# Seven of 22 up-projection pairs as seven products, low parts of weights partly by DMA, and the down projection's weight sums made earlier

## The chip, the cores and the metric

The kernel runs on one core of a Trainium2 chip. The metric is device time in microseconds (us) of one execution. A core has five engines that run their own instruction streams side by side: TensorE (PE, matrix products), VectorE (DVE), ScalarE (ACT), GpSimd (POOL) and SyncE (SP, here only the issuer of loads). They wait for one another by semaphores. Data moves between memory (DRAM) and the on-chip buffers by 16 DMA engines; SP, ACT and POOL issue such transfers, each on its own queue. A PE product lands in one of eight banks of the accumulation memory.

## The reference

One layer of an encoder: x is 512 tokens of 1024 numbers in float32, with 256 memory tokens. Cut to its steps:

```python
h = rmsnorm(x, pre_mix_g)
aq, ak, av, hq, hf_fwd, hf_bwd, hi, hg = split_columns(h @ w_in, IN_SPLITS)
att = axial_gqa_attention(apply_rope(rmsnorm(aq, q_norm_g)), apply_rope(rmsnorm(ak, k_norm_g)), av)
rec = hgrn2_group(hq, hf_fwd, hf_bwd, hi, hg, lb, hg_out_norm_g)   # a scan over the tokens, both directions
x = x + rmsnorm(concatenate([att, rec]) @ w_out, post_mix_g)
h, m = rmsnorm(x, pre_x_g), rmsnorm(mem, mem_norm_g)
x = x + rmsnorm(memory_cross_attention(h, m, w_xq, w_xkv, w_xo), post_x_g)
u = rmsnorm(x, pre_ffn_g) @ w_up                                   # 1024 -> 2 * 2816
gate, val = split(conv_b + sum(pad(u)[j:j + 512] * conv_w[j] for j in range(3)))
x = x + rmsnorm((silu(gate) * val) @ w_down, post_ffn_g)           # 2816 -> 1024
```

## The kernel before

**Products in three.** Every float32 product is made of three matmuls in the format float32r. An operand is split into a high part (a cast) and a low part (the rest); `mm3` (L242 to L245) multiplies high by high, high by low and low by high into one bank. `split` (L117 to L119) makes the two parts: an ACT cast (L118) and a DVE subtraction (L119).

**Weights come in units.** A unit is a block of 128x1024 numbers (512 KB); there are 162, numbered in the order in which PE uses them. Units 0 to 65 belong to the token mixing and the cross attention, 66 to 119 to the up projection, 120 to 161 to the down projection. `load_w` issues a unit's load on SP. `issue` makes the unit's high part `wh` and low part `wl`, up to three units ahead of use (AHEAD); each has four buffers, so a unit's parts can be made only when the unit four places earlier has been used. Most low parts are DVE subtractions. For units 7 to 30 (NEG_SCALAR) ACT writes the negated high part into `wl` (L214), and POOL issues a DMA that adds the weight to it from memory (L217). For units 31 to 41 (NEG_POOL) POOL does the negation (L216).

**Attention.** The token mixing runs a scan over chunks of tokens on DVE (L633, L639), ACT (L604) and PE (L607, bank c), and between its steps the planner puts products of the attention. `turn_k` (L711 to L716) transposes the keys of one block of 128 tokens on PE into a bank with the tag b and has ACT cast the result out (L716). The attention projection's products use bank b too. A tag stands for two banks that take turns.

**Residual and norm.** `between` (L309 to L325) adds a sub-layer's normed output to x, norms the sum and hands back a call of `turn_in` (L278 to L289), which transposes the result on PE and splits it for the next projection. Before the up projection it also keeps an unsplit copy of each transposed block in `fulls` (ACT, L289).

**Up projection.** The 22 pairs of a gate block and a value block run in a loop over i. A plain pair is two units, each 24 matmuls of 128x512. A pair named in UP_S uses a scheme of seven half-size products in place of eight (Strassen's): 84 matmuls of 128x256. It takes four units: `diag` and `side` are loaded, `sums` and `last` are sums of blocks of these made by `add_blocks` on DVE, where `both` holds the double sum. The left operands are sums of the halves of h, made by `sum_of_h` from `fulls` during pairs 2 and 3.

**Down projection.** It uses seven products p = 0 to 6 as well, with six units each. Four of the seven weights are sums of blocks of w_down (t1 to t4). `new_sums` (L988 to L999) makes them in DRAM, at every third pair of the up projection: a copy of the first block (on ACT's queue L997 or POOL's L994) and an adding DMA of the second (L998, POOL). The loads for the down projection wait for them. The left operands are the products of gate and value, in three groups g of eight pairs or six; `left_side` (L1010 to L1027) splits the operand of product p for group g, either on ACT and DVE, or, for the (p, g) in NEG_GROUP, by an ACT cast (L1022), a POOL negation (L1023) and an adding DMA between on-chip buffers (L1024). For p = 3 a DVE subtraction (L1014) first overwrites what the earlier operand was split from. `order` runs through p and, within it, g; LAY_AHEAD = 3 of them are laid ahead.

A tile framework places the buffers and semaphores: an instruction waits until its inputs are written and until the earlier users of its output's buffer are done.

Of the kernel before, what the change touches and what calls it, by code (L numbers as in the profile page):

```python
# [9 lines left out]
F32 = mybir.dt.float32  # L10
# [8 lines left out]
P = 128  # L19
# [9 lines left out]
UP_S = (5, 8, 11, 14, 17)  # L29
# [6 lines left out]
SUMS = (("t1", "w11", "w12"), ("t3", "w22", "w12"), ("t2", "t1", "w22"), ("t4", "t2", "w21"))  # L36
BLOCKS = ("w11", "w12", "w21", "w22")
UP_PRODUCTS = ("w11", "w22", "t2", "w21", "t1", "t3", "t4")
LAY_AHEAD, LOAD_AHEAD = 3, 5
SIDES_AT = (18, 19)  # L40
NEG_GROUP = frozenset((p, 1) for p in (1, 2, 5, 6))
# [3 lines left out]
NEG_SCALAR = frozenset(range(7, 31))  # L45
# [41 lines left out]
def layer(tc, io, out):  # L87
# [42 lines left out]
    issued, loaded, taken, last_load, rooms = [0], [0], [0], [None], [0]  # L130
# [12 lines left out]
    whole = N_MIX  # L143
    for i in range(NF):
        if i in UP_S:
            plan += [(kind, UP_S.index(i)) for kind in ("diag", "side", "sums", "last")]
        else:
            plan += [("w", whole), ("w", whole + 1)]
            whole += 2
# [16 lines left out]

    def load_w():
        i = loaded[0]
        loaded[0] += 1
        if i >= N_DOWN:  # L170
            p, u = divmod(i - N_DOWN, 6)
            cols = width(u)
            raw = raw_room(i)[:, :cols.stop - cols.start]
            src = weight_block(PRODUCTS[p][0], cols)
        else:
            kind, n = plan[i]
            if kind in ("sums", "last"):
                return None
            raw = raw_room(i)
            src = io["w"][n] if kind == "w" else io["wu"][n, ("diag", "side").index(kind)]  # L180
        last_load[0] = nc.sync.dma_start(raw, src).ins
        return raw

    def add_blocks(kind, raw, ahead):
        if kind == "diag":
            both = vp.tile([P, 1024], F32, name="both", tag="vv")
            mid = ahead[:, :512]
            nc.vector.tensor_tensor(out=both.rearrange("p (a n) -> p a n", a=2), in0=raw.rearrange("p (a n) -> p a n", a=2),
                                    in1=mid[:, None, :].to_broadcast([P, 2, 512]), op=ALU.add)
# [8 lines left out]
    def issue():  # L198
# [12 lines left out]
        if i in NEG_SCALAR or i in NEG_POOL:  # L211
            nc.scalar.copy(wh, raw)  # L212
            if i in NEG_SCALAR:
                nc.scalar.mul(wl, wh.bitcast(F32), -1.0)  # L214
            else:
                nc.gpsimd.tensor_scalar(wl, wh.bitcast(F32), -1.0, 0.0, op0=ALU.mult, op1=ALU.add)  # L216
            nc.gpsimd.dma_start(wl, io["w"][i], accum_op=ALU.add)  # L217
        else:
            split(wh, wl, raw)
            add_blocks(kind, raw, raws[0] if raws else None)  # L220
        pending.append((wh, wl))

    hold = [N_UNITS]

    def issue_ahead():
        while issued[0] < min(hold[0], taken[0] + AHEAD):
            issue()
        while N_MIX + 4 <= taken[0] and loaded[0] < min(N_UNITS, taken[0] + LOAD_AHEAD):
            raws.append(load_w())
# [48 lines left out]
    def turn_in(h, act, b, tags, keep=None):  # L278
        for c in range(2):
# [8 lines left out]
            if keep:  # L288
                nc.scalar.copy(keep[c][:, :, blk(b)], o)  # L289
# [19 lines left out]
    def between(x, g_post, g_pre, act, keep=None):  # L309
# [4 lines left out]
        def second(b, got, y):  # L314
# [9 lines left out]
            return lambda: turn_in(h, act, b, y_tags[0][b] + y_tags[1][b], keep)  # L324
# [83 lines left out]
    nhalf = const.tile([P, 16], F32, name="nhalf")  # L408
    warm = tmp2()
# [301 lines left out]
    def turn_k(b):  # L711
        o = bank("b").rearrange("p (k n) -> p k n", k=4)
# [270 lines left out]
    fulls = [big([P, 4, T]) for _ in range(2)]  # L983
    turns = res_second(ox, range(4), kv["x0"], between(x, g_post, g_pre, hT, fulls))
# [78 lines left out]
    for part in range(2):  # L1063
        cols = slice(part * 256, part * 256 + 256)
        for n in range(4):
# [10 lines left out]
    of_h = [(s1, a21, a22), (s2, a11, s1), (s3, a21, a11), (s4, a12, s2)]  # L1076

# [47 lines left out]
    for i in range(2, NF):  # L1125
        if i in UP_S:
            strassen_pair(i)
        else:
            for c in range(2):
# [183 lines left out]
```

## Time and profile before

| | us |
|---|---|
| median of 3 runs | 825.16 |
| the three runs | 825.16, 825.99, 824.77 |
| profiled execution | 825.72 |
| its span, first to last instruction | 823.8 |

The granted PE clock was 0.999 of full speed. The time of a run is about 1.9 us longer than the span that the trace covers; positions below are us from the span's start. In rows of the trace the columns are: start, duration, engine, line of the kernel, operation, output<-input, shape, and in brackets the idle time of the engine before it with what ended that. A row of the list of waits has the waiting engine, its output and line, what it waited for, and total us, number and longest. A row of busy time by stage has, for a stretch of the span, the busy us of PE, PE's weight loads, DVE, ACT and POOL (with the number of instructions), the granted PE clock, the busy share of the DMA engines and GB/s. In a row of the costliest groups the number behind an x counts the instructions, and then come their busy us and the mean ns of one. The up projection runs from about 484 to 709 us, the down projection from 709 to 816.

### The profile page before, as it was taken

How to read it: one execution, taken by the hardware profiler on the slowest of the kernel's cores; microseconds unless marked ns; L12 is line 12 of the kernel's file. 1: busy time of each engine (PE TensorE's matmuls, PEld its weight loads, DVE VectorE, ACT ScalarE, POOL GpSimd, SP SyncE). 2: the span in 40 equal slices, each digit the busy share in tenths (PEclk: the TensorE clock that was granted, in tenths of full speed). 3: DMA queues.
4: the chain of work that ended last, by engine and by line, in shares of the span. 5: the costliest groups of instructions: out<-in, count | busy, mean ns of one | idle time of the engine just before them, and what ended most of it. 6: DMA issues, size and time to landing. Idle time of an engine off the chain costs nothing.

```text
span 823.8 us, 11495 instructions
## 1 busy us (share of the span) xinstructions
PE 808.1 (98%) x4354; PEld 690.6 (84%) x4354; DVE 568.5 (69%) x849; ACT 473.0 (57%) x785; POOL 132.3 (16%) x194
## 2 busy tenths in 40 slices
PE   9999999999999999999999999999999999999996
PEld 7878888889898887888888898889889888878884
DVE  5347486569886875855453769787687796868865
ACT  6666756369788874645543665444344453556651
POOL 0110211044233101300001300111110102100302
PEclk9999999999999999999999999999999999999999
DMA  9696753657668533252212145787898885368842
GB/s 316 186 283 134 173 112 95 129 140 162 160 155 191 116 136 120 77 179 78 88 43 101 37 163 153 205 232 202 224 279 217 232 250 146 103 200 295 249 124 102
DMA packets 39671, 135.66 MB, mean 165 GB/s; under 512 B 5120, under 2 KB 6656, under 8 KB 39424
## 3 DMA queue, kind: packets, MB, share of 16 engines
q1 hardware_dynamic: 25632, 86.03, 30.0%
q0 software_dynamic: 10960, 40.38, 25.5%
q10 hardware_dynamic: 3024, 8.53, 2.9%
q8 instruction: 34, 0.56, 0.3%
q14 instruction: 21, 0.17, 0.1%
HBM read 130.72 MB, written 25.17 MB: 189 GB/s over the span
## 4 chain that ended last, share of the span: by engine, by line
PE 84%; DMA 4%; DVE 4%; issue 3%; ACT 2%; POOL 2%; SPq 0%; POOLq 0%; DVEq 0%; ACTq 0%
PE ps_b L243 9%; PE ps_b L244 9%; PE ps_b L245 9%; PE ps_s L244 6%; PE ps_s L245 6%; PE ps_s L243 6%; PE ps_o L243 5%; PE ps_o L245 5%; PE ps_o L244 5%; PE ps_c L245 4%; PE ps_c L244 4%; PE ps_c L243 4%; PE ps_c L607 3%; PE ps_o L851 2%; PE ps_s L830 2%
## 5 line engine op out<-in xcount | busy, mean ns | idle before, releaser
L119 DVE TENSOR_TENSOR wl<-raw,wh 128x1024 fp32r<-128x1024 f32 (+1 forms) x75 | 90.7, 1212 | 64.1 <-ACT wh L118 63.8
L118 ACT CAST wh<-raw 128x1024 fp32r<-128x1024 f32 (+1 forms) x75 | 76.8, 1027 | 83.0 <-PE ps_b L244 25.7
L243 PE MATMUL ps_b<-big,wh 128*128 128x512 f32 (+1 forms) x340 | 122.4, 360 | 0.7 <-DVE big L119 0.7
L245 PE MATMUL ps_b<-big,wl 128*128 128x512 f32 (+1 forms) x340 | 120.5, 355 | 0.0
L244 PE MATMUL ps_b<-big,wh 128*128 128x512 f32 (+1 forms) x340 | 120.5, 354 | 0.0
L243 PEld LDWEIGHTS ps_b<-big,wh 128*128 128x128 f32 x340 | 64.3, 189 | 9.2 <-DVE big L119 0.9
L244 PEld LDWEIGHTS ps_b<-big,wh 128*128 128x128 f32 x340 | 64.3, 189 | 8.6
L245 PEld LDWEIGHTS ps_b<-big,wl 128*128 128x128 f32 x340 | 64.2, 189 | 8.7
L633 DVE TENSOR_TENSOR big<-big 128x512 f32<-128x512 f32 x64 | 48.4, 761 | 16.4 <-PE ps_c L607 10.1
L244 PE MATMUL ps_s<-wl,big 128*128 128x512 f32 (+1 forms) x140 | 53.4, 381 | 2.6 <-DVE wl L119 1.7
L243 PE MATMUL ps_s<-wh,big 128*128 128x512 f32 (+1 forms) x140 | 53.5, 384 | 0.4 <-DVE big L119 0.4
L245 PE MATMUL ps_s<-wh,big 128*128 128x512 f32 (+1 forms) x140 | 53.1, 379 | 0.0
L212 ACT CAST wh<-raw 128x1024 fp32r<-128x1024 f32 x35 | 36.8, 1052 | 26.7 <-PE ps_b L244 12.9
L217 POOL DMA_DIRECT2D wl<-in_w_dram x35 | 30.9, 883 | 120.1 <-ACT wl L214 105.1
L119 DVE TENSOR_TENSOR big<-ps_o,big 128x512 fp32r<-128x512 f32 x54 | 37.0, 688 | 14.1 <-ACT big L118 12.2
L998 POOL DMA_DIRECT2D sum_t<-in_wd_dram x24 | 19.7, 833 | 143.7 <-DMA sum_t<-in_wd_dram 86.8
L118 ACT CAST big<-ps_o 128x512 fp32r<-128x512 f32 x54 | 31.6, 589 | 17.2 <-PE ps_o L953 7.5
L243 PE MATMUL ps_o<-wh,big 128*128 128x512 f32 (+1 forms) x102 | 39.3, 386 | 0.0
L244 PE MATMUL ps_o<-wl,big 128*128 128x512 f32 (+1 forms) x102 | 38.2, 375 | 0.0
L245 PE MATMUL ps_o<-wh,big 128*128 128x512 f32 (+1 forms) x102 | 38.2, 374 | 0.0
L244 PE MATMUL ps_c<-big,wh 128*128 128x256 f32 (+1 forms) x112 | 37.6, 336 | 0.0
L243 PE MATMUL ps_c<-big,wh 128*128 128x256 f32 (+1 forms) x112 | 37.6, 336 | 0.0
(311 smaller groups left out, 2171.0 us busy)
## 6 DMA issues: line engine op xcount, KB each, us to landing
raw<-in_w_dram SPq DMA_DIRECT2D x85, 512.0 KB, 3.3
wl<-in_w_dram POOLq DMA_DIRECT2D x35, 512.0 KB, 5.4
sum_t<-in_wd_dram POOLq DMA_DIRECT2D x20, 512.0 KB, 8.1
tmp<-in_w_dram SPq DMA_DIRECT2D x14, 512.0 KB, 6.0
sum_t<-in_wd_dram ACTq DMA_DIRECT2D x10, 512.0 KB, 6.2
sum_t<-sum_t POOLq DMA_DIRECT2D x10, 512.0 KB, 5.2
big<-sum_t SPq DMA_DIRECT2D x10, 512.0 KB, 4.9
raw<-sum_t SPq DMA_DIRECT2D x10, 512.0 KB, 4.5
```

Source lines behind the costliest of these rows:

```text
L118: nc.scalar.copy(hi, src)
L119: (eng or nc.vector).tensor_sub(lo, src, hi.bitcast(F32))
L212: nc.scalar.copy(wh, raw)
L217: nc.gpsimd.dma_start(wl, io["w"][i], accum_op=ALU.add)
L243: nc.tensor.matmul(o, a[0], b[0], start=start, stop=False, skip_group_check=again)
L244: nc.tensor.matmul(o, a[0], b[1], start=False, stop=False, skip_group_check=again)
L245: last_mm[0] = nc.tensor.matmul(o, a[1], b[0], start=False, stop=stop, skip_group_check=again).ins
L607: nc.tensor.matmul(o[:, b, :], kc[:, blk(b)], pat(qk, b * P, [[2 * m, P // (2 * m)], [T + m, 2], [1, m]]), start=True, stop=True)
L633: nc.vector.tensor_tensor(out=c, in0=c, in1=pat(tt, toff + off, [[2, npair], [gap, 2], [0, m]]), op=ALU.mult)
L830: nc.tensor.matmul(s, qT[h // 4][:, h % 4, blk(qb)], kT[:, 2 * (h // 4) + c, :], start=c == 0, stop=c == 1)
L851: nc.tensor.matmul(o, vv[:, c, h // 4].rearrange("p a d -> p (a d)"), pt[j][:, c, :], start=c + j == 0, stop=c == 3 and j == 1)
L998: nc.gpsimd.dma_start(t, weight_block(second_name, width(u)), accum_op=ALU.add)
```

## The change

- **UP_S** names seven pairs in place of five: 5, 7, 9, 11, 13, 15, 17 (before 5, 8, 11, 14, 17).
- **Low parts.** The whole low part of a `diag` unit and the second half of a `side` unit's are made by an ACT negation and an adding DMA (LOW_FROM). `both` is ordered behind the last low part that DVE made (`issue_after(last_low)`). Units 7 and 8 leave NEG_SCALAR; DVE makes their low parts.
- The number of units grows from 162 to 166, since such a pair has four in place of two.
- **Loads** in the up projection go seven units ahead in place of five; in the down projection five, as before.
- **The down projection's sums** are no longer made in one place. 24 seeds (copies of a first block) go on SP's queue behind the raw loads of units 28 to 45 and 60 to 65. 24 adds go on POOL's queue, each behind a copy of one column of a unit's low part (`mark`), at units 52 to 59 and then with the plain pairs of the up projection. t2 and t4 are added up in another order, and the DRAM tiles are 32 columns wider.
- **turn_k** uses the banks of `tm_tags`, which are s, s, o, o for the four blocks.
- **fulls** is made by DVE from the split parts (`full_h`) at pair 2; the copies at L289 go, and `sum_of_h` runs four times at pair 3.
- **NEG_GROUP**: (0, 1) takes the place of (1, 1).

Line numbers in the rows of the changed kernel below are its own: its L749 is L715 of before, L278 to L280 are L243 to L245, L230 is L217, L1043 is L1022, L1060 is L1039, and L222 and L121 are the casts.

PE, where the keys of the first blocks are transposed. Before, bank b only (`big` is the keys' block, `tmp` a matrix of the scan, `wh` and `wl` a weight unit):

```order
L715 MATMUL ps_b<-ident_r,big 128x128 x4
L607 MATMUL ps_c<-big,tmp_1932 128x128 x4
L715 MATMUL ps_b<-ident_r,big 128x128 x4
L243 MATMUL ps_b<-big,wh 128x256
L244 MATMUL ps_b<-big,wh 128x256
```

The same place now:

```order
L749 MATMUL ps_s<-ident_r,big 128x128 x6
L641 MATMUL ps_c<-big,tmp_1937 128x128 x4
L749 MATMUL ps_s<-ident_r,big 128x128 x2
L278 MATMUL ps_b<-big,wh 128x256
L279 MATMUL ps_b<-big,wh 128x256
```

The transposes go to bank s, and bank b is left to the projection's products.

POOL, in the middle of the up projection. Before, the DRAM sums of one step (`sum_t` with the number of the unit in it):

```order
L998 DMA sum_t_3_5650<-in_wd_dram 128x1024
L998 DMA sum_t_3_5653<-in_wd_dram 128x1024
L994 DMA sum_t_3_5656<-sum_t_3_5650 16x8192
L998 DMA sum_t_3_5656<-in_wd_dram 128x1024
L994 DMA sum_t_3_5659<-sum_t_3_5656 16x8192
L998 DMA sum_t_3_5659<-in_wd_dram 128x1024
```

POOL now, in the same part:

```order
L230 DMA wl<-in_wu_dram 128x1024
L230 DMA wl<-in_wu_dram 128x512
L236 COPY mark<-wl 128x1
L251 DMA sum_t_3_3020<-sum_t_3_1968 128x1024
L230 DMA wl<-in_wu_dram 128x1024
L230 DMA wl<-in_wu_dram 128x512
```

The low parts of a diag and a side unit now stand on this queue, with one add behind a mark between two such pairs.

ACT, at the end of the up projection and the start of the down projection. Before (`tmp` and `cw` belong to the convolution of pairs 20 and 21, `big` holds the left sides, `raw` a weight):

```order
L1039 ACTIVATE tmp_6533<-ps_b,cw 128x512
L118 CAST big<-big 128x1024
L118 CAST wh<-raw 128x1024
L118 CAST wh<-raw 128x512
L1022 CAST big<-big 128x1024
L118 CAST wh<-big 128x1024 x2
L118 CAST big<-big 128x768
```

ACT now, from the step of pair 21's gate on:

```order
L1060 ACTIVATE tmp_6653<-ps_s,cw 128x512
L1043 CAST big<-big 128x1024
L121 CAST big<-big 128x768
L1066 ACTIVATE tmp_6653<-tmp_6653 128x512
L222 CAST wh<-big 128x1024
L1060 ACTIVATE tmp_6689<-ps_c,cw 128x512
```

The cast that is followed by a POOL negation and a DMA (L1022, now L1043) stands before the last convolution steps: it is that of (0, 1), no longer that of (1, 1).

The diff:

```diff
@@ -28,3 +28,3 @@
 EPS = 1e-6
-UP_S = (5, 8, 11, 14, 17)
+UP_S = (5, 7, 9, 11, 13, 15, 17)
 N_MIX, N_WHOLE = 66, 110 - 2 * len(UP_S)
@@ -35,8 +35,11 @@
 PRODUCTS = (("w11", "b"), ("t2", "s"), ("t1", "c"), ("w22", "o"), ("t3", "s"), ("t4", "c"), ("w21", "b"))
-SUMS = (("t1", "w11", "w12"), ("t3", "w22", "w12"), ("t2", "t1", "w22"), ("t4", "t2", "w21"))
+SUMS = (("t1", "w11", "w12"), ("t3", "w22", "w12"), ("t2", "w22", "t1"), ("t4", "w21", "t2"))
 BLOCKS = ("w11", "w12", "w21", "w22")
 UP_PRODUCTS = ("w11", "w22", "t2", "w21", "t1", "t3", "t4")
-LAY_AHEAD, LOAD_AHEAD = 3, 5
+LAY_AHEAD, LOAD_AHEAD = 3, (7, 5)
 SIDES_AT = (18, 19)
-NEG_GROUP = frozenset((p, 1) for p in (1, 2, 5, 6))
+LOW_FROM = {"diag": 0, "side": 512}
+SEEDS_AT = frozenset(range(28, 46)) | frozenset(range(60, 66))
+ADDS_AT = frozenset(range(52, 60))
+NEG_GROUP = frozenset((p, 1) for p in (0, 2, 5, 6))
 AHEAD = 3
@@ -44,3 +47,3 @@
 TURN_STEP, MEM_TURN, UP_TURN = 0, (0, 4), (0, 2)
-NEG_SCALAR = frozenset(range(7, 31))
+NEG_SCALAR = frozenset(range(9, 31))
 NEG_POOL = frozenset(range(31, 42))
@@ -129,3 +132,3 @@
     pending, last_pow, last_mm = deque(), [None], [None]
-    issued, loaded, taken, last_load, rooms = [0], [0], [0], [None], [0]
+    issued, loaded, taken, last_load, last_low, rooms = [0], [0], [0], [None], [None], [0]
 
@@ -142,3 +145,3 @@
     plan = [("w", i) for i in range(N_MIX)]
-    whole = N_MIX
+    whole, adds_at = N_MIX, set(ADDS_AT)
     for i in range(NF):
@@ -147,2 +150,4 @@
         else:
+            if i >= 2:
+                adds_at.update((len(plan), len(plan) + (i - 1 not in UP_S)))
             plan += [("w", whole), ("w", whole + 1)]
@@ -166,2 +171,6 @@
 
+    def source(i):
+        kind, n = plan[i]
+        return io["w"][n] if kind == "w" else io["wu"][n, ("diag", "side").index(kind)]
+
     def load_w():
@@ -175,7 +184,6 @@
         else:
-            kind, n = plan[i]
-            if kind in ("sums", "last"):
+            if plan[i][0] in ("sums", "last"):
                 return None
             raw = raw_room(i)
-            src = io["w"][n] if kind == "w" else io["wu"][n, ("diag", "side").index(kind)]
+            src = source(i)
         last_load[0] = nc.sync.dma_start(raw, src).ins
@@ -187,4 +195,6 @@
             mid = ahead[:, :512]
-            nc.vector.tensor_tensor(out=both.rearrange("p (a n) -> p a n", a=2), in0=raw.rearrange("p (a n) -> p a n", a=2),
-                                    in1=mid[:, None, :].to_broadcast([P, 2, 512]), op=ALU.add)
+            with tc.issue_after(last_low[0]):
+                nc.vector.tensor_tensor(out=both.rearrange("p (a n) -> p a n", a=2),
+                                        in0=raw.rearrange("p (a n) -> p a n", a=2),
+                                        in1=mid[:, None, :].to_broadcast([P, 2, 512]), op=ALU.add)
             nc.vector.tensor_add(mid, both[:, :512], raw[:, half(1)])
@@ -210,13 +220,38 @@
             wh, wl = wh[:, :raw.shape[1]], wl[:, :raw.shape[1]]
-        if i in NEG_SCALAR or i in NEG_POOL:
-            nc.scalar.copy(wh, raw)
-            if i in NEG_SCALAR:
-                nc.scalar.mul(wl, wh.bitcast(F32), -1.0)
-            else:
+        by_dma = 0 if i in NEG_SCALAR or i in NEG_POOL else LOW_FROM.get(kind, raw.shape[1])
+        nc.scalar.copy(wh, raw)
+        if by_dma:
+            last_low[0] = nc.vector.tensor_sub(wl[:, :by_dma], raw[:, :by_dma], wh[:, :by_dma].bitcast(F32)).ins
+        if by_dma < raw.shape[1]:
+            if i in NEG_POOL:
                 nc.gpsimd.tensor_scalar(wl, wh.bitcast(F32), -1.0, 0.0, op0=ALU.mult, op1=ALU.add)
-            nc.gpsimd.dma_start(wl, io["w"][i], accum_op=ALU.add)
-        else:
-            split(wh, wl, raw)
-            add_blocks(kind, raw, raws[0] if raws else None)
+            else:
+                nc.scalar.mul(wl[:, by_dma:], wh[:, by_dma:].bitcast(F32), -1.0)
+            nc.gpsimd.dma_start(wl[:, by_dma:], source(i)[:, by_dma:], accum_op=ALU.add)
+        add_blocks(kind, raw, raws[0] if raws else None)
         pending.append((wh, wl))
+        if i in SEEDS_AT:
+            seeds.popleft()()
+        if i in adds_at and adds:
+            with tc.issue_after(nc.gpsimd.tensor_copy(mark, wl[:, 0:1].bitcast(F32)).ins):
+                adds.popleft()()
+
+    seeds, adds = deque(), deque()
+
+    def plan_sums(out_name, first_name, second_name, u):
+        n = width(u).stop - width(u).start
+
+        def seed():
+            t = dram.tile([P, n + 32], F32, name="sum_%s_%d" % (out_name, u), tag="sum_%s_%d" % (out_name, u))[:, :n]
+            sums.setdefault(out_name, []).append(t)
+            with tc.issue_after(last_load[0]):
+                nc.sync.dma_start(t, weight_block(first_name, width(u)))
+
+        seeds.append(seed)
+        adds.append(lambda: nc.gpsimd.dma_start(sums[out_name][u], weight_block(second_name, width(u)),
+                                                accum_op=ALU.add))
+
+    for names in SUMS:
+        for u in range(6):
+            plan_sums(*names, u)
 
@@ -227,3 +262,3 @@
             issue()
-        while N_MIX + 4 <= taken[0] and loaded[0] < min(N_UNITS, taken[0] + LOAD_AHEAD):
+        while N_MIX + 4 <= taken[0] and loaded[0] < min(N_UNITS, taken[0] + LOAD_AHEAD[loaded[0] >= N_DOWN]):
             raws.append(load_w())
@@ -277,3 +312,3 @@
 
-    def turn_in(h, act, b, tags, keep=None):
+    def turn_in(h, act, b, tags):
         for c in range(2):
@@ -287,4 +322,2 @@
                 split(hi[0][:, c * 4:c * 4 + 4, blk(b)], lo[0][:, c * 4:c * 4 + 4, blk(b)], o)
-            if keep:
-                nc.scalar.copy(keep[c][:, :, blk(b)], o)
 
@@ -308,3 +341,3 @@
 
-    def between(x, g_post, g_pre, act, keep=None):
+    def between(x, g_post, g_pre, act):
         def first(b, y):
@@ -323,3 +356,3 @@
                 scale_rows(x[b], ss[:, R:R + 1], g_pre, h, c)
-            return lambda: turn_in(h, act, b, y_tags[0][b] + y_tags[1][b], keep)
+            return lambda: turn_in(h, act, b, y_tags[0][b] + y_tags[1][b])
         return first, second
@@ -408,2 +441,3 @@
     nhalf = const.tile([P, 16], F32, name="nhalf")
+    mark = const.tile([P, 1], F32, name="mark")
     warm = tmp2()
@@ -711,3 +745,3 @@
     def turn_k(b):
-        o = bank("b").rearrange("p (k n) -> p k n", k=4)
+        o = bank(tm_tags[b]).rearrange("p (k n) -> p k n", k=4)
         kd4 = qkv["kd"][:, b].rearrange("p a b c d -> p (a b) (c d)")
@@ -982,4 +1016,3 @@
     hT = new_act()
-    fulls = [big([P, 4, T]) for _ in range(2)]
-    turns = res_second(ox, range(4), kv["x0"], between(x, g_post, g_pre, hT, fulls))
+    turns = res_second(ox, range(4), kv["x0"], between(x, g_post, g_pre, hT))
 
@@ -988,14 +1021,2 @@
 
-    def new_sums(u):
-        n = width(u).stop - width(u).start
-        for out_name, first_name, second_name in SUMS:
-            t = dram.tile([P, n], F32, name="sum_%s_%d" % (out_name, u), tag="sum_%s_%d" % (out_name, u))
-            if first_name in sums:
-                nc.gpsimd.dma_start(t, weight_block(first_name, width(u)))
-            else:
-                with tc.issue_after(last_act[0]):
-                    nc.scalar.dma_start(t, weight_block(first_name, width(u)))
-            nc.gpsimd.dma_start(t, weight_block(second_name, width(u)), accum_op=ALU.add)
-            sums.setdefault(out_name, []).append(t)
-
     def group_sides(g):
@@ -1071,2 +1092,3 @@
                 turns.popleft()()
+    fulls = [big([P, 4, T]) for _ in range(2)]
     wide = [big([P, 2, 4, 256]) for _ in range(2)]
@@ -1077,2 +1099,5 @@
 
+    def full_h(k):
+        nc.vector.tensor_add(fulls[k], hT.hi[k].bitcast(F32), hT.lo[k].bitcast(F32))
+
     def sum_of_h(k):
@@ -1134,6 +1159,8 @@
                 conv(c, i, o)
-                if i < 4:
-                    sum_of_h(2 * i - 4 + c)
-        if i % 3 == 2 and i // 3 < 6:
-            new_sums(i // 3)
+                if i == 2:
+                    full_h(c)
+                elif i == 3:
+                    sum_of_h(2 * c)
+                    sum_of_h(2 * c + 1)
+    assert not seeds and not adds
 
```

More of the change, by code (lines that the diff above doesn't have):

```diff
@@ L210, in issue @@
             wh, wl = wh[:, :raw.shape[1]], wl[:, :raw.shape[1]]
-        if i in NEG_SCALAR or i in NEG_POOL:
-            nc.scalar.copy(wh, raw)
-            if i in NEG_SCALAR:
-                nc.scalar.mul(wl, wh.bitcast(F32), -1.0)
-            else:
-                nc.gpsimd.tensor_scalar(wl, wh.bitcast(F32), -1.0, 0.0, op0=ALU.mult, op1=ALU.add)
-            nc.gpsimd.dma_start(wl, io["w"][i], accum_op=ALU.add)
-        else:
-            split(wh, wl, raw)
-            add_blocks(kind, raw, raws[0] if raws else None)
-        pending.append((wh, wl))
+        by_dma = 0 if i in NEG_SCALAR or i in NEG_POOL else LOW_FROM.get(kind, raw.shape[1])
[4 more added lines that the diff above has]
+            if i in NEG_POOL:
+                nc.gpsimd.tensor_scalar(wl, wh.bitcast(F32), -1.0, 0.0, op0=ALU.mult, op1=ALU.add)
+            else:
+                nc.scalar.mul(wl[:, by_dma:], wh[:, by_dma:].bitcast(F32), -1.0)
+            nc.gpsimd.dma_start(wl[:, by_dma:], source(i)[:, by_dma:], accum_op=ALU.add)
+        add_blocks(kind, raw, raws[0] if raws else None)
+        pending.append((wh, wl))
+        if i in SEEDS_AT:
[17 more added lines that the diff above has]
+            plan_sums(*names, u)
     hold = [N_UNITS]
```

## The prediction

> **What bounds the kernel now.** I read the page's first part, then the list of PE's waits, then the rows around each wait, then busy time by stage.
>
> ```profile
> span 823.8 us, 11495 instructions
> PE 808.1 (98%) x4354; PEld 690.6 (84%) x4354; DVE 568.5 (69%) x849; ACT 473.0 (57%) x785; POOL 132.3 (16%) x194
> ```
>
> PE is busy 98% of the span and no other engine more than 69%. So the time changes in two ways only: PE gets fewer or shorter matmuls, or PE's few stops go or new ones come. The list of waits names the stops (engine, line, what it waited for, total, times, longest):
>
> ```profile
> PE ps_s L244 <- DVE wl L119: 1.7, 1, 1.7
> ...
> PE ps_s L244 <- DMA wl<-in_w_dram: 1.0, 1, 1.0
> PE ps_b L243 <- DVE big L119: 0.7, 1, 0.7
> PE ps_b L715 <- ACT big L716: 0.7, 2, 0.5
> PE ps_o L243 <- ACT big L289: 0.6, 1, 0.6
> ...
> PE ps_c L282 <- ACT big L289: 0.5, 1, 0.5
> ```
>
> These six rows are 5.2 us, and the change touches the cause of each. A stop costs a little more than its idle time, as two neighbouring rows show:
>
> ```profile
> 50.14 0.39 PE L243 MATMUL ps_s<-wh,big 128*128 128x512 f32 x1
> 51.52 0.50 PE L244 MATMUL ps_s<-wl,big 128*128 128x512 f32 x1 [0.98 <-DMA wl<-in_w_dram]
> ```
>
> Start to start this is 1.38 us, where an undisturbed 128x512 matmul follows the one before it after 0.23 (708.86 to 709.09 below). So 0.98 idle cost 1.15. I add 0.2 to each stop.
>
> **Two more seven-product pairs.** The first such pair and the plain pair behind it:
>
> ```profile
> 527.95 0.28 PE L243 MATMUL ps_c<-big,wh 128*128 128x256 f32 x1
> ...
> 538.01 0.40 PE L243 MATMUL ps_s<-big,wh 128*128 128x512 f32 x1
> ...
> 548.92 0.39 PE L243 MATMUL ps_o<-big,wh 128*128 128x512 f32 x1
> ```
>
> The seven-product pair (84 matmuls of 128x256) takes 538.01 − 527.95 = 10.06 us, the plain one (48 of 128x512) 10.91. The gain is 0.85 a pair, **−1.7 us** for two. That is 0.120 and 0.227 us a matmul; half the columns cost more than half the time, so an eighth fewer multiplications becomes 8%. The Trainium skill ("TensorE: Matmul & The Clock Gate", "Wait — 56ns, not 53.3ns?") gives N / 2.4 GHz plus about 2.5 ns; by it the two pairs would gain an estimated 2.4 us. The rows here are slower for both shapes, and I keep the rows.
>
> **Units 7 and 8.** PE's stop at 51.52 is for unit 8's low part, which comes by a cast, a negation and an accumulating DMA:
>
> ```profile
> 40.23 1.03 ACT L212 CAST wh<-raw 128x1024 fp32r<-128x1024 f32 x1
> ...
> 41.70 1.04 ACT L214 ACTIVATE wl<-wh 128x1024 fp32r<-128x1024 f32 x1
> ```
> ```profile
> 43.06 0.85 POOL L217 DMA_DIRECT2D wl<-in_w_dram  x1 [5.01 <-ACT wl L214]
> ```
> ```profile
> 36.00:60.00 24.00, 23.02 (x108) 18.91 (x106) 8.19 (x15) 18.15 (x25) 3.63 (x4) 1.00 0.98 274
> ```
> ```profile
> L119 DVE TENSOR_TENSOR wl<-raw,wh 128x1024 fp32r<-128x1024 f32 x71 | 86.7, 1222 | 63.9 <-ACT wh L118 63.6
> ```
>
> From the issue at 43.06 to PE's start at 51.52 are 8.46 us, with the DMA engines 98% busy. After the change DVE does the subtraction right behind the cast: 1.22 us, on an engine busy 8.19 of the 24 us. The low part is there near 41.3 + 1.2 = 42.5. Without the stop: **−1.2**. Unit 9 is now first on the slow road; it gains a quieter DMA queue and nothing earlier. If its DMA were slower by several us the stop would return, which sets the bound at 0.
>
> **Keys' transposes in other banks.** Two stops on L715 and one on `ps_b L243` come from sharing bank b with the attention projection's products: 0.7 + 0.7 idle, three stops, 1.4 + 3 × 0.2 = 2.0 us at most. But DVE is nearly full here, and PE waits on its scan chain too:
>
> ```profile
> 196.00:217.00 21.00, 19.15 (x159) 18.39 (x158) 19.70 (x52) 17.54 (x34) 10.12 (x15) 1.00 0.92 215
> ```
>
> DVE has 21.00 − 19.70 = 1.3 us free. If the freed PE runs into DVE, only that much can be won; the bounds are 0 and −2.0. I take **−1.3**.
>
> **Keep copies.** Eight ACT copies (L289) go. One of them, and the stops at L282 and L243 behind them:
>
> ```profile
> 478.42 0.59 ACT L289 COPY big<-ps_c 128x512 f32<-128x512 f32 x1 [1.60 <-DVE big L119]
> ```
>
> ACT stood 1.60 us behind DVE before a copy that nothing urgent needs. PE's two stops are 0.5 + 0.6 idle and 0.4 of restart: **−1.5**, if nothing takes their place (bounds −0.5 and −1.5: the rms chain through ACT, POOL and DVE is still there). DVE does the work instead: two 128x2048 additions, about 2 × 2.4 = 4.9 us by the 1.22 for 128x1024, early in the up projection:
>
> ```profile
> 481.00:528.00 47.00, 47.00 (x265) 41.37 (x265) 38.37 (x44) 25.72 (x33) 3.10 (x4) 1.00 0.60 175
> ```
>
> ```profile
> 519.93 1.22 DVE L119 TENSOR_TENSOR big<-big 128x1024 fp32r<-128x1024 f32 x1
> ```
>
> DVE has 8.6 us free there and PE stops nowhere. The second row is the low part of the last of the four sums of h, ready at 521.15; 4.9 later is 526.1. Its product is the second of the first seven-product pair, 12 matmuls behind 527.95: 529.4. I cost it at nothing; the 3.3 us are the cover, and beyond them each us costs one.
>
> **Down projection's sums, seeds and marks.** The same 24 sums move to other queues and earlier. The 24 seeds stand on SP behind raw loads, the adds on POOL, each behind a copy of one column. SP's next raw load waits behind a seed's issue. Two stages show the room:
>
> ```profile
> 345.00:420.00 75.00, 75.00 (x394) 64.03 (x393) 41.64 (x61) 37.50 (x80) 2.96 (x5) 1.00 0.32 114
> ...
> 560.00:666.00 106.00, 106.00 (x626) 94.59 (x625) 81.22 (x106) 48.25 (x61) 15.34 (x22) 1.00 0.84 226
> ```
>
> The DMA engines are 32% busy where many seeds and adds go, 84% in the up projection they leave. PE stops in neither stage. Zero, with a bound of about +1 if a raw load behind a seed comes late by more than its unit waits now.
>
> **Diag and side low parts by DMA.** Seven diag units (512 KB) and half of seven side units go the same road as unit 8. In steady state a diag unit's buffer is freed when PE ends the third unit of the pair before: 527.95 + 72 × 0.12 = 536.6. Behind that pair's last product and a plain pair the unit's first low product would start near 548.92 + 0.24 = 549.2. The room is 12.6 us. The chain is cast 1.03, negation 1.04, POOL's 0.3 to issue and the DMA:
>
> ```profile
> DMA to landing us min/median/max: 5.1/5.4/10.4
> ```
>
> By the median it ends 4.8 us early, by the longest of 35 it is 0.2 us late. So zero, with a rival below. DVE loses 1.2 + 0.7 us a pair, which nothing waits for.
>
> **Down projection: which left sides go by DMA.** PE's largest stop, 1.7 at `ps_s L244`, came from left side (1,1): its chain, and the subtraction that held up DVE until the DMA had read its source:
>
> ```profile
> 716.50 1.04 ACT L1022 CAST big<-big 128x1024 fp32r<-128x1024 f32 x1
> ```
> ```profile
> 717.64 1.94 POOL L1023 TENSOR_SCALAR big<-big 128x1024 fp32r<-128x1024 f32 x1 [17.22 <-ACT big L1022]
> 719.88 0.90 POOL L1024 DMA_DIRECT2D big<-big  x1 [0.30 <-POOL big L1023]
> ```
> ```profile
> 728.36 1.23 DVE L1014 TENSOR_TENSOR big<-big 128x1024 f32<-128x1024 f32 x1 [4.83 <-DMA big<-big]
> ...
> 730.37 1.22 DVE L119 TENSOR_TENSOR wl<-raw,wh 128x1024 fp32r<-128x1024 f32 x1
> ```
>
> DVE sat 4.83 us, so the weight's low part at 730.37 came late. With (1,1) on DVE (1.22 us) the wait goes: 1.7 + 0.2 = **−1.9**.
>
> In its place (0,1) now takes the DMA. Its buffer comes free where it does today, at the cast of 706.34, and the first down product starts at 709.09:
>
> ```profile
> 706.34 1.79 ACT L118 CAST big<-big 128x1024 fp32r<-128x1024 f32 x2 [0.99 <-PE ps_b L244]
> ```
> ```profile
> 708.86 0.39 PE L245 MATMUL ps_b<-big,wl 128*128 128x512 f32 x1
> 709.09 0.39 PE L243 MATMUL ps_b<-wh,big 128*128 128x512 f32 x1
> ```
> ```profile
> DMA to landing us min/median/max: 7.1/8.4/11.3
> ```
>
> Cast to 707.4, POOL's negation 1.05 to 1.94 from 707.5 on, 0.3 to the issue: about 708.9. The four DMAs of this kind took 7.1 to 11.3 us; by the median's 8.4 it lands at 717.3. PE needs the low part at the fifth of the eleven row blocks, 24 matmuls and two more behind 709.09: 709.1 + 26 × 0.227 = 715.0. PE is in order, so it stands: **+2.2**, bounds 0 and +5.9 (11.3 us and the longer negation).
>
> **Sum**: −1.7 − 1.2 − 1.3 − 1.5 − 1.9 + 2.2 = −5.4. The profiled execution took 825.72 (span 823.8 and 1.9 around it), 0.56 above the median of 825.16. So 820.3 for such an execution, and **819.8** against the median, which I predict.
>
> **The rivals.**
> - No stop at the first down product. A DMA of the same kind in a quiet moment needs only the 5.1 us of the weights' shortest: landing at 714.0, before 715.0. Then 819.8 − 2.2 = 817.6. For it: few loads run just then. Against: all four of this kind took 7.1 or more. The Trainium skill ("DMA: Bandwidth & Descriptors", "Anatomy of one DMA — SWDGE (gpsimd) path") fits 2.0 us plus bytes / 436e3; 512 KB is an estimated 3.2 us, and by it this stop does not come. The trace disagrees: none of the 39 accumulating DMAs of that size into on-chip buffers was under 5.1 us.
> - The won time is given back: bank b's 1.3 stays lost to DVE's scan, or (0,1) takes 11.3 us. The first gives 821.1, the second 819.8 + 3.7 = 823.5, half of both about 822.5.
> - Slower: the diag units' DMA comes late. Its mechanism is the 12.6 us of room; it decides from a landing of 12.6 − 2.4 = 10.2 us on. Each us beyond costs PE one us in each of the six pairs behind the first. At 11.9 us that is 6 × 1.7 = 10.2 and 830.0. For it: the longest took 10.4, and the queue holds a side unit's DMA and an add beside it. Against: the median of 5.4, and less DMA traffic in this stage, since all seeds and 8 of the 24 adds run before it.
> - The sums don't leave the stage in time, or seeds delay a raw load: about +1 each, inside the second rival.
>
> **How the numbers follow.** The forecast, 818.2 to 821.5, gets 0.48; the first rival 0.17; the second 0.20 (821.5 to 824); the third 0.08 above 826.8; 0.07 is left for no measurable difference by several small losses. Within 0.2% (1.65 us, about what a measurement of this kernel can tell from no change) means 823.5 to 826.8: the 0.07 and a fifth of the second rival, 0.11. Faster: 0.81. The range, 816.8 to 824.0, takes in the first two rivals and leaves out the third.
>
> **What would show it.** The list of waits after should have no `wl<-in_w_dram` near 51, no L715 row's successor, no stop near 480 and none behind the subtraction for p = 3. It should have one new wait of about 2 us, on the DMA from `big` to `big`, some 6 us into the down projection. Pairs 7 to 17 should take 10.1 us each with no wait on `wl<-in_wu_dram`; PE's share between 530 and 700 should stay whole. I am wrong if a wait on `wl<-in_wu_dram` repeats once per pair, or if DVE's scan stage is as long as before.

## The result and the profile after

The changed kernel takes **832.71 us** (median of 4 runs, 831.44 to 835.77), the kernel before 825.06 in the same comparison: a ratio of 1.0095, 95% interval 1.0069 to 1.0121. It is slower by 0.95%, where 819.8 was predicted with a range up to 824.0. The profiled execution took 831.84.

The page's first part, of the changed kernel:

```profile
span 830.1 us, 11789 instructions
PE 808.7 (97%) x4426; PEld 694.4 (84%) x4426; DVE 574.6 (69%) x866; ACT 480.0 (58%) x795; POOL 138.5 (17%) x218
```

The span is 6.3 us longer. PE has less to do (72 matmuls more, since twice 84 of 256 columns stand where twice 48 of 512 stood), and yet its busy time rose from 808.1 to 808.7. Part of the loss is therefore not idle time. The list of PE's waits, columns as before:

```profile
PE ps_b L278 <- DVE big L955: 3.8, 1, 3.8
PE ps_b L280 <- DMA big<-big: 2.9, 1, 2.9
PE ps_o L278 <- DVE tmp L1137: 1.6, 1, 1.6
PE ps_b L279 <- DVE big L122: 1.3, 1, 1.3
...
PE ps_c L278 <- ACT tmp L1135: 0.4, 1, 0.4
...
PE ps_s L864 <- ACT big L750: 0.3, 1, 0.3
```

All six stops that the prediction set out to remove are gone or down to 0.3 (L750 is the keys' cast). Five new rows took over, at three places: near 370 (3.8), in the first seven-product pair (1.6, 1.3 and 0.4) and at the first down product (2.9). The last is the one that was forecast.

Matching PE rows show where the time moves. Of the kernel before (the scan's end, the attention's):

```profile
131.84 0.50 PE L243 MATMUL ps_s<-wh,big 128*128 128x512 f32 x1 [0.39 <-DVE big L119]
...
252.67 0.33 PE L840 MATMUL ps_o<-ident,tmp 128*128 128x128 f32 x1 [0.18 <-ACT tmp L816]
```

Of the changed kernel, the same two, then the start of the first seven-product pair, its end, and the first down product:

```profile
130.38 0.50 PE L278 MATMUL ps_s<-wh,big 128*128 128x512 f32 x1 [0.37 <-DVE big L122]
...
249.43 0.33 PE L874 MATMUL ps_o<-ident,tmp 128*128 128x128 f32 x1 [0.17 <-ACT tmp L850]
...
530.07 0.28 PE L278 MATMUL ps_c<-big,wh 128*128 128x256 f32 x1
...
544.24 0.40 PE L278 MATMUL ps_s<-big,wh 128*128 128x512 f32 x1
...
713.74 0.39 PE L278 MATMUL ps_b<-wh,big 128*128 128x512 f32 x1
```

The changed kernel is 1.46 ahead at the first, 3.24 ahead at the second, 2.12 *behind* at 530.07 (527.95 before), 6.23 behind at 544.24 (538.01 before) and 4.65 behind at 713.74 (709.09 before). So it loses 5.4 between the attention's end and the first pair, 4.1 inside that pair, and wins 1.6 in the rest of the up projection.

**The stop near 370.** Rows of POOL, ACT and PE of the changed kernel:

```profile
355.08 0.94 POOL L251 DMA_DIRECT2D sum_t<-in_wd_dram  x1
...
358.16 0.82 POOL L251 DMA_DIRECT2D sum_t<-in_wd_dram  x1 [0.26 <-issue]
```
```profile
367.34 1.04 ACT L222 CAST wh<-raw 128x1024 fp32r<-128x1024 f32 x1 [8.11 <-DMA raw<-in_w_dram]
368.29 0.59 ACT L954 ACTIVATE big<-ps_b 128x512 fp32r<-128x512 f32 x1
```
```profile
370.30 0.80 PE L278 MATMUL ps_b<-big,wh 128*128 128x512 f32 x1 [3.83 <-DVE big L955]
370.89 0.63 PE L279 MATMUL ps_b<-big,wh 128*128 128x512 f32 x1
```

The list of waits blames DVE, and DVE only passes the wait on. Its subtraction needs ACT's cast of the query block at 368.29. That cast stood behind the cast of a weight unit, which waited 8.11 us for its raw load. The list of DMA issues of the changed kernel from 357 to 360.6 says how long the transfers took (last column, median us to landing):

```profile
raw<-in_w_dram SPq DMA_DIRECT2D x2, 512.0 KB, 10.1
sum_t<-in_wd_dram POOLq DMA_DIRECT2D x1, 512.0 KB, 9.5
```

The same list of the kernel before, 357 to 361:

```profile
raw<-in_w_dram SPq DMA_DIRECT2D x2, 512.0 KB, 3.2
```

A raw load took 10 us in place of 3.2 with two of the moved adds under way.

**The clock behind it.** From 370.30 to 370.89 are 0.59 us for one 128x512 matmul, where 0.23 was usual. Busy time of 371 to 376 and 377 to 380:

```profile
371.00:376.00 5.00, 5.00 (x20) 4.54 (x19) 2.00 (x3) 1.54 (x2) 1.08 (x3) 0.50 0.91 182
377.00:380.00 3.00, 3.00 (x17) 2.55 (x16) 1.34 (x5) 2.05 (x10) 0.00 (x0) 1.00 1.05 285
```

The granted clock is 0.50 for about 6 us behind the stop. Six us at half clock do the work of three: some 3 us of busy time without use, on top of the 4.0 of the stop.

Matching PE rows on both sides of the place, of the kernel before and then of the changed one:

```profile
360.06 0.39 PE L243 MATMUL ps_b<-big,wh 128*128 128x512 f32 x1
...
375.20 0.39 PE L243 MATMUL ps_b<-big,wh 128*128 128x512 f32 x1
```
```profile
356.79 0.39 PE L278 MATMUL ps_b<-big,wh 128*128 128x512 f32 x1
...
378.75 0.39 PE L278 MATMUL ps_b<-big,wh 128*128 128x512 f32 x1
```

From one to the other are 15.14 us before and 21.96 now: this place costs 6.8.

**The first seven-product pair.** ACT and DVE of the changed kernel, 30 us ahead of it:

```profile
503.29 1.05 ACT L222 CAST wh<-raw 128x1024 fp32r<-128x1024 f32 x1 [6.24 <-DMA raw<-in_w_dram]
```
```profile
504.38 1.22 DVE L224 TENSOR_TENSOR wl<-raw,wh 128x1024 fp32r<-128x1024 f32 x1 [5.30 <-ACT wh L222]
```

Again a cast waits for its raw load, with adds of pairs 2 and 3 beside it, and the convolution's step behind the cast (and DVE behind that) waits along. DVE loses 5.3 us, more than the 3.3 us of cover. The last sum of h comes late, and PE stops three times: 1.3 for that sum, then 0.4 and 1.6 for steps of the pair itself on ACT and DVE.

**The first down product.** The wait is on the DMA of left side (0, 1). ACT's cast, and the summary of the DMA's line:

```profile
710.99 1.06 ACT L1043 CAST big<-big 128x1024 fp32r<-128x1024 f32 x1 [0.99 <-PE ps_c L279]
```
```profile
DMA to landing us min/median/max: 6.3/8.8/10.3
```

### The profile page after: what moved, and what is told of

Its sections match the earlier page's. It is cut to its first block, busy times and chain, and to the rows that moved or that the text cites. A ratio compares the mean times of both kernels' runs of the same rounds, so it can differ in the third digit from the quotient of the medians.

```text
span 830.1 us, 11789 instructions
## 1 busy us (share of the span) xinstructions
PE 808.7 (97%) x4426; PEld 694.4 (84%) x4426; DVE 574.6 (69%) x866; ACT 480.0 (58%) x795; POOL 138.5 (17%) x218
## 3 DMA queue, kind: packets, MB, share of 16 engines
q10 hardware_dynamic: 1296, 2.76, 1.0%
## 5 line engine op out<-in xcount | busy, mean ns | idle before, releaser
L222 ACT CAST wh<-raw 128x1024 fp32r<-128x1024 f32 x110 | 113.7, 1035 | 124.3 <-PE ps_b L279 30.6
L224 DVE TENSOR_TENSOR wl<-raw,wh 128x1024 fp32r<-128x1024 f32 (+1 forms) x70 | 80.0, 1145 | 73.8 <-ACT wh L222 73.7
L278 PE MATMUL ps_b<-big,wh 128*128 128x512 f32 (+1 forms) x344 | 122.5, 356 | 3.8 <-DVE big L955 3.8
L280 PE MATMUL ps_b<-big,wl 128*128 128x512 f32 (+1 forms) x344 | 120.6, 350 | 0.0
L278 PEld LDWEIGHTS ps_b<-big,wh 128*128 128x128 f32 x344 | 65.3, 190 | 12.0 <-DVE big L955 4.2
L279 PEld LDWEIGHTS ps_b<-big,wh 128*128 128x128 f32 x344 | 65.4, 190 | 9.3 <-DVE big L122 1.5
L280 PEld LDWEIGHTS ps_b<-big,wl 128*128 128x128 f32 x344 | 65.2, 190 | 8.2
L278 PE MATMUL ps_s<-wh,big 128*128 128x512 f32 (+1 forms) x140 | 53.3, 382 | 0.4 <-DVE big L122 0.4
L280 PE MATMUL ps_s<-wh,big 128*128 128x512 f32 (+1 forms) x140 | 53.1, 379 | 0.0
L230 POOL DMA_DIRECT2D wl<-in_w_dram x33 | 29.0, 878 | 121.0 <-ACT wl L229 106.0
L224 DVE TENSOR_TENSOR wl<-tmp,wh 128x1024 fp32r<-128x1024 f32 (+1 forms) x25 | 26.8, 1073 | 23.3 <-ACT wh L222 23.3
L222 ACT CAST wh<-tmp 128x1024 fp32r<-128x1024 f32 (+1 forms) x25 | 23.2, 928 | 32.2 <-PE ps_o L279 8.9
L121 ACT CAST big<-ps_o 128x512 fp32r<-128x512 f32 x54 | 31.7, 588 | 16.9 <-PE ps_o L987 7.5
L278 PE MATMUL ps_c<-big,wh 128*128 128x256 f32 (+1 forms) x120 | 40.0, 333 | 0.4 <-ACT tmp L1135 0.4
L279 PE MATMUL ps_c<-big,wh 128*128 128x256 f32 (+1 forms) x120 | 39.9, 333 | 0.0
L280 PE MATMUL ps_c<-big,wl 128*128 128x256 f32 (+1 forms) x120 | 39.9, 332 | 0.0
L278 PE MATMUL ps_o<-wh,big 128*128 128x512 f32 (+1 forms) x102 | 39.5, 387 | 0.0
L278 PE MATMUL ps_s<-big,wh 128*128 128x256 f32 (+1 forms) x116 | 39.0, 336 | 0.0
```

The lines of the kernel that those rows point to most:

```text
L121: nc.scalar.copy(hi, src)
L224: last_low[0] = nc.vector.tensor_sub(wl[:, :by_dma], raw[:, :by_dma], wh[:, :by_dma].bitcast(F32)).ins
L230: nc.gpsimd.dma_start(wl[:, by_dma:], source(i)[:, by_dma:], accum_op=ALU.add)
L278: nc.tensor.matmul(o, a[0], b[0], start=start, stop=False, skip_group_check=again)
L279: nc.tensor.matmul(o, a[0], b[1], start=False, stop=False, skip_group_check=again)
L280: last_mm[0] = nc.tensor.matmul(o, a[1], b[0], start=False, stop=stop, skip_group_check=again).ins
```

## The experiments

Theory A says that the moved adds stretch the raw loads beside them, that ACT takes its work in order, and that what stands behind the waiting cast is late. Each of the first three kernels mends one of the three places, the fourth mends all.

**Adds at other units.**

```diff
-ADDS_AT = frozenset(range(52, 60))
+ADDS_AT = frozenset(range(58, 66))
```

> Eight adds move from units 52 to 59 to units 58 to 65; the rest is the changed kernel. Theory A (adds that run beside the raw loads of units 55 and 56 stretch these from 3.3 to about 10 us, and ACT, which takes its work in order, holds the queries' casts behind them): no stop of 3.8 us near 370, no half clock behind it, 6.9 us less, so near 825.5. The stops near 533 to 540 stay at 4 us. Rival B (PE arrives earlier there than before, and the loads would be late without the adds too): the stop stays, no change from 832.

Measured 829.12 (826.37 to 831.06), ratio 1.0049, interval 1.0025 to 1.0072. Its list of waits:

```profile
PE ps_b L280 <- DMA big<-big: 2.8, 1, 2.8
PE ps_c L641 <- ACT tmp L638: 2.4, 1, 2.4
PE ps_o L278 <- DVE tmp L1137: 1.6, 1, 1.6
```

The stop near 370 is gone, so B falls. The sum was missed by 3.6. In the profiled execution the reason is the second row: a stop of 2.4 near 63, in a stretch of the program that this edit does not touch. It is not in the profiled execution of the changed kernel. It is taken up below. One more thing was missed: the first pair was to lose 4 us as before, and its stop of 1.3 is gone too. In this execution the value block's raw load of pair 3 took 7.3 us in place of 9.1, DVE stood 3.50 in place of 5.30, and the pair is 1.8 shorter, which bears theory A out.

**No adds at pairs 2 to 4.**

```diff
-            if i >= 2:
+            if i >= 6:
-ADDS_AT = frozenset(range(52, 60))
+ADDS_AT = frozenset(range(52, 66))
```

> The six adds at pairs 2 to 4 of the up projection move to units 60 to 65; those at units 52 to 59 stay. Theory A: the raw load of the value block of pair 3 takes 3.3 in place of 9.1 us, DVE's idle time of 5.3 us near 500 goes, and so do the stops of 3.4 us idle in the first seven-product pair: 4.1 less than the changed kernel, near 828.5, with the 6.9 near 370 still there. Rival C (DVE is overfull there by the two additions of 4.6 us and the four sums at one pair, with or without the adds): the stops stay above 2 us.

Measured 830.99 (827.89 to 833.10), ratio 1.0071, interval 1.0047 to 1.0095. Its list of waits begins:

```profile
PE ps_b L278 <- DVE big L955: 3.9, 1, 3.9
PE ps_b L280 <- DMA big<-big: 2.8, 1, 2.8
PE ps_c L641 <- ACT tmp L638: 2.3, 1, 2.3
```

No stop of the first pair is left in it (the smaller rows behind are at other places). C falls: the two additions and four sums on DVE fit, once ACT doesn't hold the engine up. The time is 2.5 above the expectation, with the early stop in it as well.

**Left side (0, 1) on DVE.**

```diff
-NEG_GROUP = frozenset((p, 1) for p in (0, 2, 5, 6))
+NEG_GROUP = frozenset((p, 1) for p in (2, 5, 6))
```

> Left side (0, 1) goes back to DVE, the rest is the changed kernel. The stop of 2.9 us at the first down product goes and nothing takes its place, since DVE has 3 to 4 us in 15 free there: 3.1 less, near 829.5. Rival: DVE gets to the low part late, a stop of about 1 stays: near 830.5.

Measured 831.99 (829.89 to 833.35), ratio 1.0087, interval 1.0062 to 1.0112. No wait on `big<-big` or elsewhere near the first down product is in its list. But the early stop of 1.8 is, and one of 4.3 near 373, so the median alone would have said that this edit is worth 0.7. The rows say 3.1.

**All three.** Adds at 42 to 44, at 57 to 65 and from pair 6 on, and (0, 1) on DVE.

> All three together: adds at units 42 to 44, 57 to 65 and from pair 6 of the up projection on, none at pairs 2 to 4; left side (0, 1) on DVE. Theory A: 832 - 6.9 - 4.1 - 3.1 = 818, faster than before by 0.8%. If B or C hold, 822 to 829.

Measured 821.69 (819.00 to 822.91), ratio 0.9957, interval 0.9942 to 0.9973: faster than before, and 3.7 above the expectation. Of the new stops only the early one is left. What each edit is worth at its place, apart from the medians, can be read from matching PE rows in front of the place and behind it (positions of the changed kernel):

| From row to row, us | before | changed kernel | that place mended alone | all three |
|---|---|---|---|---|
| 356.79 to 378.75 | 15.14 | 21.96 | 15.14 | 15.14 |
| 530.07 to 544.24 | 10.06 | 14.17 | 10.07 | 10.05 |
| 713.74 to 731.93 | 15.07 | 18.19 | 14.96 | 14.96 |

Each edit gives back what its place had lost. ACT and PE of the kernel with all three, at the early stop:

```profile
62.76 0.69 ACT L705 ACTIVATE big<-big,rx 128x128 f32<-128x128 f32 x2 [4.53 <-DMA big<-in_rope_dram]
63.36 0.60 ACT L638 COPY tmp<-big 128x512 f32<-128x512 f32 x1
```
```profile
64.01 1.22 PE L641 MATMUL ps_c<-big,tmp 128*128 128x128 f32 x4 [2.93 <-ACT tmp L638]
```

It is the same pattern with other names. The step that prepares the rotary tables (L705) waits for its load, and the scan's copy (L638) that PE needs stands behind it. In the order of ACT before, all four parts of this step stood behind the fourth copy of the scan. In the changed kernel two of them stand before the third; in its profiled execution L705 stood only 1.33 us for the load, and PE did not stop there. Theory D: this is a by-product of taking units 7 and 8 off ACT.

**Tables first**, otherwise as all three:

```diff
-        mem_load()
         load_tables()
+        mem_load()
```

> As the three together (e4), and the rotary tables are loaded ahead of the memory tokens. Theory D (with units 7 and 8 on DVE, the rotary step stands between the scan's steps on ACT, waits there for its tables, and holds up the scan's copies that PE needs): the stop of 1.8 to 2.9 us near 62 to 64 and the half clock behind it (1.7 us) go, 4.8 less than e4: near 817. Rival: it is the scan itself that is late, the stop stays and the time is that of e4, 821.7.

Measured **818.31** (818.01 to 819.56), ratio 0.9921, interval 0.9907 to 0.9935; that lies clear of the interval without this edit. Its list of waits is down to stops at places that the change doesn't touch, and one of 0.3 at the keys' cast:

```profile
PE ps_b L466 <- DVE tmp L447: 1.3, 1, 1.3
PE ps_s L505 <- ACT wh L481: 0.9, 2, 0.6
PE ps_c L641 <- DVE big L667: 0.6, 2, 0.4
```

The span is 816.4, 7.4 less than before. The five gains of the prediction add up to 7.6. By the rows of the changed kernel they came to 8.3 (see below), so that the sum agrees better than its terms do.

**Units 7 and 8 back on the slow road** (NEG_SCALAR from 7, otherwise as all three):

> As e4, and units 7 and 8 get their low parts by DMA again. Theory D: the rotary step moves behind the scan's steps again, no stop near 64; the stop of 1.0 us near 51 comes back, 1.2 to 1.4 in all: near 818.3. Rival (the rotary step is early for another reason): both stops, near 823.

Measured 819.70 (817.53 to 820.41), ratio 0.9933, interval 0.9918 to 0.9947. ACT's order has the rotary step behind the scan's copies again and there is no stop near 64, so D holds as to the cause. The stop near 51 did not come back in this execution: the low part landed in time. That half of the expectation was missed. The profiled execution is the fastest of the six, by 2.0; what the other five did there is not on record.

**Low parts on DVE** (LOW_FROM empty, otherwise as tables first):

> As e6, and the low parts of diag and side units are made by DVE. If DVE has room for 1.9 us more per 21 us (it is busy some 12 of 15 us there): no stop in the pairs, and the time of e6 within 1 us. Rival (that part of the change is what makes seven pairs possible): DVE falls behind in pairs 7 to 17, stops of 0.5 us or more at each, 3 us or more above e6.

Measured 817.78 (817.27 to 818.76), ratio 0.9915, interval 0.9901 to 0.9929: the same as with the DMAs. Busy time from 560 to 666, of tables first and of this kernel:

```profile
560.00:666.00 106.00, 106.00 (x666) 96.33 (x665) 84.92 (x118) 57.81 (x74) 15.32 (x25) 1.00 0.65 166
```
```profile
560.00:666.00 106.00, 106.00 (x667) 96.33 (x666) 91.38 (x123) 50.62 (x67) 8.18 (x16) 1.00 0.45 128
```

DVE goes from 84.9 to 91.4 of 106 us, and PE stops in neither. So the low parts by DMA brought nothing here, and cost nothing.

**Seven pairs alone**, in the kernel before:

```diff
-UP_S = (5, 8, 11, 14, 17)
+UP_S = (5, 7, 9, 11, 13, 15, 17)
```

> The kernel before with nothing but seven pairs in place of five. By the rows of the two pairs 1.7 less than before, 823.3. If DVE or the sums' DMA can't keep up with pairs at every second place, stops in the pairs eat it: 825 or more.

Measured 824.92 (822.50 to 827.18 in 12 runs), ratio 0.9989, interval 0.9971 to 1.0007: no difference. Two rows of its list of waits are new, both in seven-product pairs:

```profile
PE ps_b L243 <- DVE tmp L1112: 0.9, 1, 0.9
...
PE ps_c L243 <- DVE tmp L1112: 0.7, 1, 0.7
```

In this execution the up projection behind the first seven-product pair is 0.9 longer than before, and not 1.7 shorter: 172.0 us from 538.38 to 710.39, by matching PE rows, where before it was 171.1. The span is 0.7 shorter all the same, because the stop of 1.7 for p = 3 is missing, though its code is as before: its DMA landed in 4.7 us in place of 8.5. So that stop does not come in every execution.

What DVE waited for is in its own list of waits and in its rows:

```profile
DVE both L188 <- DMA raw<-in_wu_dram: 10.8, 5, 3.5
```
```profile
551.58 1.22 DVE L188 TENSOR_TENSOR both<-raw 128x1024 f32<-128x1024 f32 x1 [3.50 <-DMA raw<-in_wu_dram]
...
556.37 0.42 DVE L1112 TENSOR_TENSOR tmp<-ps_b,tmp 128x256 f32<-128x256 f32 x1
```

The double sum (L188) waits for its raw load, which took 7.3 us beside copies of the down projection's sums, and L1112, for which PE stops at 556.85, stands behind it on DVE. Before, this wait is 0.3 in all. So the two pairs need another part of the change. Low parts by DMA are not it (the kernel before this one). In the changed kernel such a load takes 7.9 us in the median, and still the one issued at 546.76 lands 7.5 us before its double sum starts. That points at the loads seven ahead and the later double sum, more than at the sums' move; no run takes these apart.

**Tables first alone**, in the changed kernel:

> The changed kernel with nothing but the rotary tables loaded ahead of the memory tokens. Theory D: executions with the stop near 62 (up to 4.8) no longer occur, and the spread of 831 to 836 closes to its lower end: 831 to 832, with the stops near 370, 535 and 722 all still there. Rival (the spread comes from the other stops): median and spread as for the changed kernel.

Measured 831.81 (829.59 to 833.49), ratio 1.0082, interval 1.0066 to 1.0098, which overlaps with the changed kernel's. The spread did not close, and that part of the expectation was wrong. The early stop is one source of the spread; the half clock is another, as the last section shows.

**Adds apart**, as tables first, with three adds at 52, 55 and 58:

> As e6, but three adds stand at units 52, 55 and 58, some 10 us apart, in place of 57 to 59. If it takes two adds at once to stretch a raw load to 9 us and one makes it 6 (as the rows at 373.55 and 354.80 of the changed kernel suggest), PE does not stop near 360 to 380 and the time is that of e6, 818.3 within 1. If one add alone holds a load for 9 us, a stop of about 3.8 and half clock come back for at least one of them: 822 or more.

Measured 818.52 (817.67 to 819.27), ratio 0.9924, interval 0.9911 to 0.9937. Its list of DMA issues from 357 to 361, and PE's row:

```profile
raw<-in_w_dram SPq DMA_DIRECT2D x2, 512.0 KB, 5.5
```
```profile
366.99 0.50 PE L278 MATMUL ps_b<-big,wh 128*128 128x512 f32 x1 [0.43 <-DVE big L955]
```

With a single add under way the two raw loads take 6.0 and 5.0 us (5.5 in the median) in place of 3.2 (none) or 10 (two), and the stop is 0.43. I had expected none at all.

## Why the prediction was wrong

- **Seven pairs, −1.7**: right. From 544.24 to 713.74 are 169.5 us, and 171.1 before from 538.01 to 709.09: −1.6.
- **Units 7 and 8, −1.2**: −1.46 at the scan's end in the profiled execution. But the edit moved the rotary step ahead of the scan's copies on ACT, which costs up to 2.9 of stop and as much as 1.7 of half clock in other executions. The prediction named nothing queued behind that step.
- **Keys' transposes, −1.3**: −1.8 (from −1.46 to −3.24). DVE had less of a hold on PE than its busy share suggested.
- **Keep copies, −1.5**: the stops at 479 and 481 are gone and nothing took their place. The additions that replace them fit on DVE, as forecast: the second experiment has no stop in the first pair.
- **Left sides, −1.9 and +2.2**: the old stop went, the new one came at the forecast matmul, with 2.9 in place of 2.0 idle. The cast started 4.65 later than before, as the whole part did, so the stop comes from the chain behind it, as worked out; its DMA took 9.2 us where 8.4 was taken. The third experiment removed it.
- **The sums, "zero, with a bound of about +1"**: this is the step that failed. It cost some 6.9 us near 370 and 4.1 in the first pair. The step rested on the DMA engines' mean share (32%) and on PE not stopping in the stage. Both are averages over loads that come just in time: a unit's raw load is issued when its buffer comes free and lands 3.2 us later, right when ACT wants it. What counted was the chain behind the cast. Two adds on the way made the load 10 us, ACT stood 8.11, the queries' cast stood behind it, and PE stopped 3.83. The first, second and tenth experiments show it from three sides. The prediction did ask whether a seed on SP would hold up a raw load; it did not ask what the adds on POOL's queue would do to one.
- **The price of a stop, "idle plus 0.2"**: holds up to 1.8 us. Longer stops were mostly followed by half clock, 1.4 to 3.0 us more. The prediction had no term for that.
- **The slower rival** named the wrong transfer. The diag units' DMAs were never late enough to stop PE, but with little to spare: they took 8.9 us in the median where 5.4 was taken, and up to 9.8 where the rival began at 10.2.

Summed by rows the change is −1.5 − 1.8 + 6.9 − 1.5 + 4.1 − 1.6 + 3.1 − 1.9 = +5.8 of the 6.3; the 6.9 is what remains of the 5.4 once the keep copies' −1.5 is taken out, and the rows on both sides of the place give 6.8.

## What to carry to other kernels

A transfer that is moved into a quiet stage is priced by the just-in-time loads that it will run beside, and a late load by what stands behind the instruction that waits for it on its in-order engine, not by the slack until PE needs that load's data. Bulk transfers belong where raw loads have time between them: the adds at units 57 to 65 of the kernel with tables first, where raw loads are issued 5 to 9 us apart, stop PE nowhere. Where they come some 3 us apart, two adds at a time cost 6.9 and one at a time 0.4 of a stop. When one edit takes work off an engine, look at what moves up on it and what that waits for; and since one late load can hide behind another, mend places one by one but judge each by its row, not by the median.

## What the runs showed of the hardware

PE's granted clock fell to 0.50 behind some of its stops. Of the stops in the profiled executions of the changed kernel and the experiments, those of 2.33, 2.41, 2.78, 2.80, 2.93, 3.40, 3.83, 3.88 and 4.33 us were followed by half clock, for 3.4 us or, behind those of 3.83 and 4.33, for 6.8. Those of 2.76 and 2.90 were not, and none of 1.80 or less was. Two stops of the same cause and length, 2.90 and 2.80 at the first down product, thus differ by 1.6 us. This is a source of the spread of 831 to 836: the slowest of the changed kernel's four executions, 835.77, has the lowest granted clock, 0.991, and the fastest, 831.44, the highest, 0.996.

The Trainium skill ("TensorE: Matmul & The Clock Gate", "What's actually happening") explains the clock by activity in windows of about 3.4 us that run freely. It names an idle window of about 3.4 us as the condition. The stretches of 3.4 and 6.8 us here fit one and two such windows; as to the condition, 2.33 us were enough here, and 2.90 once were not. Whether it is the place of a stop within such a window that decides is not shown by any run here.
